# A list scheduler that draws 700 varied rankings, with step times taken from the trace

## The chip, the cores and the metric

The kernel runs on one core of a Trainium2 chip. The metric is the device time of one execution in microseconds (us), as the median of several runs. One core has five engines with a program each: PE (TensorE, matmuls; its weight loads are listed as PEld), DVE (VectorE), ACT (ScalarE), POOL (GpSimd) and SP, which here only issues DMAs. An engine runs its program in the written order and stops where an instruction waits for another engine or for a DMA.

## The reference

One layer of a diffusion transformer over 256 latent tokens x and 256 context tokens ctx, all of width 2048, in fp32. Cut to what matters:

```python
sh1, sc1, g1, sh2, sc2, g2 = split(silu(c) @ w_ada + b_ada, 6)      # 2048 x 12288, for c and for c_ctx
q, k, v (two head groups)  = (x * (1 + sc1) + sh1) @ w_in           # 2048 x 3072, context tokens likewise
heads = [window attention with a sink logit, global attention]      # rotary, qk-norm, keys of latent and context
x = layer_norm(ALPHA * x + g1 * (heads @ w_out))
u = x * (1 + sc2) + sh2
x = layer_norm(ALPHA * x + g2 * ((silu(u @ w_gate) * (u @ w_up)) @ w_down))   # hidden width 5632
```

## The kernel before

Every fp32 operand of a large product is split in two: `hi`, a cast on ACT, and `lo`, the rest, a subtraction on DVE (L537 and L540 in the first part, L268 and L269 in the FFN). `mm3` (L277 to L280) then makes one product of three matmuls of 128 x 512: hi by hi (L278), weights' lo (L279), input's lo (L280). So each MB of weights costs DMA time, ACT and DVE time and PE time together.

The first part goes up to about 392 us. It holds the modulation columns from w_ada (PE matmuls L588, and for one group of columns sums on DVE, `csum`, L650 and L652), the modulated input and its turn by PE (`uf`, `uh`, `ul`), the w_in products into `qacc` and `kvacc`, the rotary turns (`qrot`, `krot`) and the flips of q and k (L967, with `kTh`, `kTl` at L929), attention, the gate row `g1b` summed on DVE (L397), the w_out products with oTh and oTl, their finish (L1255, L1258, L1261), and the second modulation (`adav` L1117, columns L1413, x flips L1443, `u2h`, `u2l`). The FFN behind it is written out in a fixed order.

The order of the first part is made by the class `Flow`. Each operation is a step with an engine, an estimated time, the steps it comes after, and the buffers it takes and gives back: 4 `raw` and 2 `araw` tiles for loads, 4 pairs for hi and lo, 4 accumulators. `forward` simulates the engines with these estimates and lets each free engine start the ready step of lowest rank, `since` being the earliest time of a step. `backward` works out how late each step could start, and these times become the ranks of the next of 8 rounds; `run` keeps the plan that ends first and then issues all steps in that plan's order. The estimates exist only there: at run time an engine waits only for what its next instruction needs.

There are 56 filler steps on PE, of two matmul records each (`warm_step`, L1276, identity by identity), of last rank, so that the plan puts them where it sees PE idle.

Of the kernel before, what the change touches and what calls it, by code (L numbers as in the profile page):

```python
# [24 lines left out]
KD = D // P  # L25
# [10 lines left out]
NB = 512  # L36
# [13 lines left out]
COLD = 3  # L50
SLACK = 2500
# [23 lines left out]
class Flow:  # L75
# [8 lines left out]
    ROUNDS = 8  # L84

# [98 lines left out]

    def run(self):
        best, end = None, math.inf
        for _ in range(self.ROUNDS):
            order, last = self.forward()
            if not order:
                break  # L190
            if last < end:
                best, end = [(s, s.start, [b.pool for b in s.take]) for s in order], last
            late = self.backward(last)
            for i, s in enumerate(self.steps):
                s.rank = (late[s], i)
        assert best, "no step can start"
        for s, s.start, pools in best:
            for b, b.pool in zip(s.take, pools):
                pass
            s.fn()  # L200
# [3 lines left out]
def dit_layer(ctx: ExitStack, tc: tile.TileContext, x, c, cx, c_ctx, w_ada, b_ada, w_in, q_norm_g,  # L204
# [250 lines left out]
    def const_tables():  # L455
        nc.gpsimd.tensor_scalar_mul(nsink, sinkb, -1.0)
        for t in range(NT):
            for g, cg, sg in ((gq, cosQ, sinQ), (gk, cosK, sinK)):
# [19 lines left out]
             {"SP": 1300.0, "PE": 5600.0, "ACT": 5000.0, "DVE": 4000.0, "POOL": 4000.0})  # L478
    pools = {"raw": wraw, "araw": araw}
# [67 lines left out]
    def flow_seed(ps, src, after):  # L547
# [6 lines left out]
        return F.add("ACT", 475, fn, after, [ps])  # L554

    def flow_products(hl, deps, ready, cols, ps, xs, first, last, prev):
# [14 lines left out]
        return F.add("PE", 688 * len(cols), fn, after, [ps] if first and not seed else [], list(hl.rooms))  # L571
# [3 lines left out]
    def flow_columns(c0, ncol, shift, scale, ats, at):  # L575
# [18 lines left out]
        for g in range(ns):  # L594
            F.at = ats[g]
            ns1 = nk / 4 * (40 + 1.67 * width)
            if not c0:
                for i, k, m, since in ((0, 0, KD, 7200.0), (1, 0, KD // 2, 9700.0), (1, KD // 2, KD // 2, 11300.0)):
# [7 lines left out]
            if c0:  # L606
# [4 lines left out]
                prev = F.add("PE", 2 * ns1 + 420, both, [l0, l1, prev], [bank] if g == 0 else [], [r0, r1])  # L611
# [24 lines left out]
    def flow_vector_columns(c0, ncol, shift, scale, ats, at):  # L636
# [17 lines left out]
        for g in range(ns):  # L654
# [9 lines left out]
            for i in range(nk):  # L664
                for s in range(2):
                    last[s] = F.add("DVE", 1215, lambda s=s, g=g, i=i, raw=raw: term(s, g, i, raw), [ld, last[s]],
# [50 lines left out]
    def flow_part(k0, n, at, each):  # L717
# [20 lines left out]
        if k0:  # L738
            for load, room in ((load_x, []), (load_cx, [cx_room])):
                a = F.add(issue, 500 if issue == "ACT" else max(ns, 500), load, take=room, since=9300.0)  # L740
                loads.append((a, -4500) if issue == "ACT" else a)
        for s in range(2):
# [3 lines left out]
            for j0 in range(0, n, 2):  # L746
# [28 lines left out]
                if k0:  # L775
                    p = F.add("PE", 205 * nj, flip, [loads[s], copy], [ps], [cx_room] if s else [])
# [52 lines left out]
    def flow_blocks(g, bs, where=("raw", "araw")):  # L829

        k0, n = GROUPS[g]
        if n == 1:
            for i, (b0, m) in enumerate(((2, 1), (0, 2), (3, 2), (5, 1))):
                F.at = bs[0] + (bs[1] - bs[0]) * i / 4
                piece, = flow_weights(w_in, k0, 1, b0 * NB, m * NB, ("b4",), since=14000.0 if i and g == 0 else 0.0)
# [54 lines left out]
    def flow_keys(w):  # L890
# [10 lines left out]
        for r in range(4):  # L901
# [36 lines left out]
            a = F.add("PE", 210, flip, [a], [ps], [rot] if r < 2 else [])  # L938
# [6 lines left out]
    def flow_queries(gi):  # L945
# [8 lines left out]
        for t in range(NT):  # L954
# [28 lines left out]
            a = F.add("PE", 400, flip, [a], [ps], [rot])  # L983
# [784 lines left out]
```

## Time and profile before

| | |
|---|---|
| median of 3 runs | 1135.83 us (1132.12 to 1136.07) |
| profiled execution | 1135.22 us |
| its span in the trace | 1133.4 us |
| granted TensorE clock, mean | 0.995 |
| PE busy | 1110.8 us, 98% |
| DVE busy | 864.6 us, 76% |
| ACT busy | 566.5 us, 50% |
| DMA | 321.26 MB, mean 283 GB/s |

The page cuts the span into 40 slices of 28.3 us. PE reads 9 tenths or more in all but the first (8) and the last (5), and DMA reads 9 or more in the first six and 7 or 8 in the next four. The chain that ended last is 80% PE, 10% DVE and 6% DMA. A row of the timeline gives start, duration, engine, line, operation, tiles, count, and in brackets the idle time just before it with what ended it.

### The profile page before, as it was taken

Reading aid. Unit: us, or ns where it says so; the run is one execution under the profiler, and the core shown is the slowest. Engines: PE = TensorE matmul, PEld = TensorE weight load, DVE = VectorE, ACT = ScalarE, POOL = GpSimd, SP = SyncE. Lnnn points to the kernel's source line nnn. Section 1 sums busy time; section 2 is a strip of 40 time slices with the busy share of each in tenths; the row PEclk is TensorE's granted clock in tenths of the full one; section 3 lists DMA queues with packets and bytes.
Section 4 is the critical chain, followed back from the end, with each engine's and each line's share of the span. In section 5 each row is a group of like instructions: output and inputs, shape, how many; then the busy total and the mean of one; then the engine's idle time right before and its main releaser. Section 6 shows DMA issues by size and latency. Waiting matters only on the chain.

```text
span 1133.4 us, 14188 instructions
## 1 busy us (share of the span) xinstructions
PE 1110.8 (98%) x5277; PEld 899.7 (79%) x5277; DVE 864.6 (76%) x1088; ACT 566.5 (50%) x820; POOL 40.4 (4%) x81
## 2 busy tenths in 40 slices
PE   8999999999999999999999999999999999999995
PEld 6766778787887688888888888888888878888884
DVE  3768998999998997877677557767767778675556
ACT  3344584877784365454564444454444443434441
POOL 1000040101200001000000000000000000000000
PEclk9999999999999999999999999999999999999998
DMA  9999998787999789989876767777777998887531
GB/s 300 383 390 397 384 347 312 247 292 244 333 337 387 279 296 346 347 294 343 282 204 223 249 223 226 247 243 249 225 244 276 312 341 285 321 278 246 194 135 74
DMA packets 186413, 321.26 MB, mean 283 GB/s; under 512 B 8764, under 2 KB 51164, under 8 KB 184039
## 3 DMA queue, kind: packets, MB, share of 16 engines
q1 hardware_dynamic: 184536, 319.25, 81.8%
q10 hardware_dynamic: 1808, 1.11, 0.4%
q8 instruction: 41, 0.67, 0.2%
q14 instruction: 28, 0.23, 0.1%
HBM read 304.07 MB, written 16.25 MB: 283 GB/s over the span
## 4 chain that ended last, share of the span: by engine, by line
PE 80%; DVE 10%; DMA 6%; issue 2%; SPq 1%; ACT 1%; DVEq 0%; ACTq 0%
PE acc L278 24%; PE acc L280 24%; PE acc L279 24%; DMA raw<-in_w_in_dram 3%; DMA raw<-in_w_ada_dram 3%; DVE lo L540 2%; PE wk L1064 2%; PE wk L588 1%; DVE csum L652 1%; DVE g1b L397 1%; SPq L514 1%; DVE adav L397 1%; DVE hx L1046 1%; PE wk L278 0%; DVE xt L1677 0%
## 5 line engine op out<-in xcount | busy, mean ns | idle before, releaser
L269 DVE TENSOR_TENSOR lo<-raw,hi 128x1024 fp32r<-128x1024 f32 x258 | 311.8, 1220 | 176.1 <-ACT hi L268 172.5
L268 ACT CAST hi<-raw 128x1024 fp32r<-128x1024 f32 x258 | 270.5, 1055 | 321.5 <-PE acc L280 279.6
L280 PE MATMUL acc<-hi,u2l 128*128 128x512 f32 x704 | 274.1, 389 | 1.2 <-DVE u2l L1592 1.2
L278 PE MATMUL acc<-hi,u2h 128*128 128x512 f32 x704 | 274.4, 390 | 0.0
L279 PE MATMUL acc<-lo,u2h 128*128 128x512 f32 x704 | 274.1, 389 | 0.0
L280 PEld LDWEIGHTS acc<-hi,u2l 128*128 128x128 f32 x704 | 132.1, 188 | 29.6 <-DVE u2l L1592 2.1
L278 PEld LDWEIGHTS acc<-hi,u2h 128*128 128x128 f32 x704 | 132.1, 188 | 28.1 <-ACT u2h L1591 0.8
L279 PEld LDWEIGHTS acc<-lo,u2h 128*128 128x128 f32 x704 | 132.2, 188 | 27.0
L537 ACT CAST hi<-raw 128x1024 fp32r<-128x1024 f32 (+1 forms) x86 | 87.7, 1033 | 95.9 <-PE acc L280 48.9
L279 PE MATMUL acc<-lo,hTh 128*128 128x512 f32 x344 | 134.0, 390 | 0.5 <-DVE lo L269 0.5
L280 PE MATMUL acc<-hi,hTl 128*128 128x512 f32 x344 | 133.9, 389 | 0.0
L278 PE MATMUL acc<-hi,hTh 128*128 128x512 f32 x344 | 133.7, 389 | 0.0
L397 DVE SCALAR_TENSOR_TENSOR adav<-raw,cs,adav 128x512 f32<-128x512 f32 (+1 forms) x128 | 121.2, 947 | 7.7 <-DMA raw<-in_w_ada_dram 5.6
L540 DVE TENSOR_TENSOR lo<-raw,hi 128x1024 fp32r<-128x1024 f32 (+1 forms) x86 | 101.3, 1194 | 16.8 <-ACT hi L537 16.6
L278 PE MATMUL acc<-hi,uh 128*128 128x512 f32 x256 | 103.4, 404 | 1.5 <-ACT qacc L821 1.4
L279 PE MATMUL acc<-lo,uh 128*128 128x512 f32 x256 | 100.1, 391 | 0.1
L280 PE MATMUL acc<-hi,ul 128*128 128x512 f32 x256 | 100.1, 391 | 0.0
L279 PEld LDWEIGHTS acc<-lo,hTh 128*128 128x128 f32 x344 | 64.6, 188 | 14.5 <-DVE lo L269 1.0
L280 PEld LDWEIGHTS acc<-hi,hTl 128*128 128x128 f32 x344 | 64.6, 188 | 13.4
L278 PEld LDWEIGHTS acc<-hi,hTh 128*128 128x128 f32 x344 | 64.5, 188 | 13.4
L278 PEld LDWEIGHTS acc<-hi,uh 128*128 128x128 f32 x256 | 48.1, 188 | 18.6 <-issue 4.6
L280 PEld LDWEIGHTS acc<-hi,ul 128*128 128x128 f32 x256 | 48.0, 188 | 10.8 <-DVE ul L772 0.4
(224 smaller groups left out, 1195.6 us busy)
## 6 DMA issues: line engine op xcount, KB each, us to landing
raw<-in_w_ada_dram SPq DMA_DIRECT2D x63, 1024.0 KB, 7.8
raw<-in_w_gate_dram SPq DMA_DIRECT2D x44, 1024.0 KB, 5.4
raw<-in_w_up_dram SPq DMA_DIRECT2D x44, 1024.0 KB, 5.6
raw<-in_w_down_dram SPq DMA_DIRECT2D x44, 1024.0 KB, 6.0
raw<-in_w_ada_dram SPq DMA_DIRECT2D x66, 512.0 KB, 6.2
raw<-in_w_in_dram SPq DMA_DIRECT2D x18, 1024.0 KB, 10.0
raw<-in_w_out_dram SPq DMA_DIRECT2D x16, 1024.0 KB, 7.8
pd<-hx SPq DMA_DIRECT2D x64, 128.0 KB, 3.8
```

The source lines that it names most:

```text
L268: nc.scalar.copy(hi[:, :n], raw[:, s : s + n])
L269: nc.vector.tensor_tensor(lo[:, :n], raw[:, s : s + n], hi[:, :n].bitcast(F32), op=ALU.subtract)
L278: nc.tensor.matmul(ps, lhsT=xh, rhs=w[0], start=first, stop=False, skip_group_check=seeded)
L279: nc.tensor.matmul(ps, lhsT=xh, rhs=w[1], start=False, stop=False, skip_group_check=seeded)
L280: nc.tensor.matmul(ps, lhsT=xl, rhs=w[0], start=False, stop=last, skip_group_check=seeded)
L397: nc.vector.scalar_tensor_tensor(a[:, c : c + piece], raw[:, f : f + piece], cs[:, 4 * (g * (G4 * NB // w) + j) + 2, None], a[:, c : c + p ...
L514: nc.sync.dma_start(room.t.rearrange("p (k n) -> p k n", k=nk), w[k0 * P : (k0 + nk) * P, c0 : c0 + width].rearrange("(k p) n -> p k n", p=P),
L537: nc.scalar.copy(hl.hi[:, :n], raw.t[:, s : s + n])
L540: nc.vector.tensor_tensor(hl.lo[:, :n], raw.t[:, s : s + n], hl.hi[:, :n].bitcast(F32), op=ALU.subtract)
L588: nc.tensor.matmul(bank.t[32 * j : 32 * j + 32, :width], lhsT=cs[:, 4 * k + 2 - 2 * i : 4 * k + 34 - 2 * i], rhs=raw.t[:, c * width : (c + ...
L652: nc.vector.scalar_tensor_tensor(a, src, cs[:, k, None], a, op0=ALU.mult, op1=ALU.add)
L1064: nc.tensor.matmul(o_ps.t[:, : 2 * P].rearrange("p (g q) -> p g q", q=32), lhsT=v, rhs=pv[:, k], start=k == 0, stop=k == 3)
```

## The change

It touches what the planner is told and how long it looks. After the 8 rounds, `run` takes the best ranks 700 times, varies those of one stretch of the plan (noise on 30% of its steps, or a common shift for one engine), plans again and keeps the plan if it ends no later than the best. Step times are set anew: the accumulator seed on ACT 475 to 519, a product 688 to 685 per block, column sums and gate sums on DVE 1215 to 1197, and so on. SP begins at 2300 and not 1300. The two halves of the second load of w_ada may start from 9900 and 11900 (before 9700 and 11300), the first casts from 16300 (before 14000), the loads of x and ctx that ACT issues from 13000 and 22000 (before 9300), and a step on SP, which issues nothing, stands for the time of such a load. No wait, no buffer and no instruction is added or removed: each engine's program holds the same instructions as before. All lines shift by 33 (L1276 is L1309, L588 is L621, L278 is L311).

```diff
+    TRIES = 700
...
+    def plan(self):
+        order, last = self.forward()
+        if order and last <= self.end:
+            self.end, self.rank = last, [s.rank[0] for s in self.steps]
+            self.best = [(s, s.start, [b.pool for b in s.take]) for s in order]
+            return True
+        return False
...
     def run(self):
...
+        draw = random.Random(SEED)
+        for _ in range(self.TRIES):
+            ranks = list(self.rank)
+            a, w, d = draw.uniform(0, self.end), draw.uniform(2e3, 4e4), draw.gauss(0, 3e3)
+            near = [i for i, r in enumerate(ranks) if a <= r <= a + w]
+            kind, e = draw.random(), draw.choice(self.ENGINES)
+            for i in near:
+                if kind < 0.6:
+                    ranks[i] += draw.gauss(0, 3e3) if draw.random() < 0.3 else 0
+                else:
+                    ranks[i] += d if self.steps[i].eng == e else 0
+            self.give_ranks(ranks)
+            if self.plan() and draw.random() < 0.3:
+                self.late_ranks(self.end)
+                self.plan()
...
-             {"SP": 1300.0, "PE": 5600.0, "ACT": 5000.0, "DVE": 4000.0, "POOL": 4000.0})
+             {"SP": 2300.0, "PE": 5600.0, "ACT": 5000.0, "DVE": 4000.0, "POOL": 4000.0})
...
-        return F.add("ACT", 475, fn, after, [ps])
+        return F.add("ACT", 519, fn, after, [ps])
...
-                a = F.add(issue, 500 if issue == "ACT" else max(ns, 500), load, take=room, since=9300.0)
-                loads.append((a, -4500) if issue == "ACT" else a)
+                a = F.add(issue, 500 if issue == "ACT" else max(ns, 500), load, take=room, since=X_FROM.get(k0, 0.0))
+                loads.append(F.add("SP", ns, lambda: None, [(a, -1000)]) if issue == "ACT" else a)
```

What moves is the order. The first place is PE's start, up to the first w_in product (`acc<-hi,uh`). The fillers are `wk<-ident`, the column matmuls `wk<-raw,cs`, the x flips `wk<-ident,xt`. Before:

```order
3 L1276 MATMUL wk<-ident 128x128 x5
4 L588 MATMUL wk<-raw,cs 32x128 x16
5 L1276 MATMUL wk<-ident 128x128 x3
...
7 L1276 MATMUL wk<-ident 128x128 x2
8 L756 MATMUL wk<-ident,xt 128x128 x2
...
11 L1276 MATMUL wk<-ident 128x128 x4
...
13 L1276 MATMUL wk<-ident 128x128 x3
14 L622 MATMUL wk<-sel,ada 128x4
15 L1276 MATMUL wk<-ident 128x128 x11
16 L278 MATMUL acc<-hi,uh 128x512
```

And with the change:

```order
3 L1309 MATMUL wk<-ident 128x128 x8
4 L621 MATMUL wk<-raw,cs 32x128 x16
...
6 L1309 MATMUL wk<-ident 128x128 x3
7 L789 MATMUL wk<-ident,xt 128x128 x2
8 L1309 MATMUL wk<-ident 128x128 x3
...
10 L1309 MATMUL wk<-ident 128x128 x12
...
12 L1309 MATMUL wk<-ident 128x128 x6
...
14 L1309 MATMUL wk<-ident 128x128 x3
15 L655 MATMUL wk<-sel,ada 128x4
16 L1309 MATMUL wk<-ident 128x128 x12
17 L311 MATMUL acc<-hi,uh 128x512
```

28 fillers stand ahead of the first product before and 47 with the change. Of the others, 20 stood in one block behind 294 products before and 8 alone; with the change 3, 1, 2, 1 and 2 stand between early products.

The second place is DVE around the last flips of k: `kTl` is what the PE flip of q behind them waits for, and `g1b` sums wait for loads of w_ada. Before:

```order
119 L397 SCALAR_TENSOR_TENSOR g1b<-raw,cs,g1b 128x1024
120 L540 TENSOR_TENSOR lo<-raw,hi 128x1024 x2
121 L397 SCALAR_TENSOR_TENSOR g1b<-raw,cs,g1b 128x1024 x3
122 L929 TENSOR_TENSOR kTl<-wk,kTh 128x2x128 x4
123 L397 SCALAR_TENSOR_TENSOR g1b<-raw,cs,g1b 128x1024
```

And with the change:

```order
132 L1009 TENSOR_TENSOR qTl<-wk,qTh 128x4x128
133 L962 TENSOR_TENSOR kTl<-wk,kTh 128x2x128
134 L430 SCALAR_TENSOR_TENSOR g1b<-raw,cs,g1b 128x1024 x2
135 L573 TENSOR_TENSOR lo<-raw,hi 128x1024
136 L962 TENSOR_TENSOR kTl<-wk,kTh 128x2x128
137 L430 SCALAR_TENSOR_TENSOR g1b<-raw,cs,g1b 128x1024
138 L573 TENSOR_TENSOR lo<-raw,hi 128x1024
139 L962 TENSOR_TENSOR kTl<-wk,kTh 128x2x128 x2
```

The four kTl no longer stand in one block behind three gate sums.

The third place is PE's end of the first part, from the last w_out products (oTh, oTl) to the first product of the FFN (u2h, u2l). Before:

```order
1303 L1117 MATMUL wk<-ones,adav 128x2 x8
1304 L278 MATMUL acc<-hi,oTh 128x512
...
1364 L1413 MATMUL wk<-raw,cs 32x512 x4
1365 L1443 MATMUL wk<-ident,xt 128x128 x4
1366 L1413 MATMUL wk<-raw,cs 32x512 x12
```

And with the change:

```order
1366 L313 MATMUL acc<-hi,oTl 128x512
1367 L1150 MATMUL wk<-ones,adav 128x2 x8
1368 L1446 MATMUL wk<-raw,cs 32x512 x4
1369 L1476 MATMUL wk<-ident,xt 128x128 x2
1370 L1446 MATMUL wk<-raw,cs 32x512 x12
1371 L311 MATMUL acc<-hi,u2h 128x512
```

The eight `adav` matmuls stood 60 products ahead of the last product; now they stand behind it, and two of the four x flips stand 12 products ahead of it.

## Rows read from the trace of the kernel before

**Rows 1.** The page: span and busy time of each engine.

```profile
span 1133.4 us, 14188 instructions
...
PE 1110.8 (98%) x5277; PEld 899.7 (79%) x5277; DVE 864.6 (76%) x1088; ACT 566.5 (50%) x820; POOL 40.4 (4%) x81
```

**Rows 2.** Waits of PE: line waited for, total, times, longest (us).

```profile
PE wk L967 <- DVE kTl L929: 2.6, 1, 2.6
PE acc L278 <- ACT qacc L821: 1.4, 1, 1.4
PE acc L280 <- DVE u2l L1592: 1.2, 1, 1.2
```

**Rows 3.** Timeline of PE, 379 to 388 us (start, us, engine, line, ...).

```profile
379.81 0.39 PE L279 MATMUL acc<-lo,oTh 128*128 128x512 f32 x1
...
387.52 0.39 PE L280 MATMUL acc<-hi,oTl 128*128 128x512 f32 x1
```

**Rows 4.** Timeline of PE, the three long gaps between neighbours.

```profile
25.99 0.39 PE L280 MATMUL acc<-hi,ul 128*128 128x512 f32 x1
27.80 0.50 PE L278 MATMUL acc<-hi,uh 128*128 128x512 f32 x1 [1.42 <-ACT qacc L821]
...
199.74 0.39 PE L280 MATMUL acc<-hi,ul 128*128 128x512 f32 x1
202.74 0.66 PE L967 MATMUL wk<-ident,qrot 128*128 128x128 f32 x4 [2.62 <-DVE kTl L929]
...
392.47 0.40 PE L279 MATMUL acc<-lo,u2h 128*128 128x512 f32 x1
394.06 0.50 PE L280 MATMUL acc<-hi,u2l 128*128 128x512 f32 x1 [1.20 <-DVE u2l L1592]
```

**Rows 5.** Timeline of PE, the first product and the filler block.

```profile
17.88 0.47 PE L278 MATMUL acc<-hi,uh 128*128 128x512 f32 x1
...
118.00 4.62 PE L1276 MATMUL wk<-ident 128*128 128x128 f32 x40
122.38 0.48 PE L278 MATMUL acc<-hi,uh 128*128 128x512 f32 x1
```

**Rows 6.** Timeline of ACT, 20 to 28 us.

```profile
26.64 0.62 ACT L537 CAST hi<-raw 128x512 fp32r<-128x512 f32 x1 [5.77 <-DMA raw<-in_w_in_dram]
```

**Rows 7.** Timeline of DVE, the column sums, 90 to 137 us.

```profile
90.85 1.42 DVE L650 TENSOR_SCALAR csum<-raw,cs 128x1024 f32<-128x1024 f32 x2 [1.53 <-DMA raw<-in_w_ada_dram]
...
127.21 9.65 DVE L652 SCALAR_TENSOR_TENSOR csum<-raw,cs,csum 128x1024 f32<-128x1024 f32 x8
136.78 1.21 DVE L540 TENSOR_TENSOR lo<-raw,hi 128x1024 fp32r<-128x1024 f32 x1
```

**Rows 8.** Timeline of SP's queue, the loads of the column sums.

```profile
82.26 1.01 SPq L387 DMA_DIRECT2D raw<-in_w_ada_dram  x2
```

**Rows 9.** Stretches of the span: us, busy by engine (x), PEclk, DMA share, GB/s.

```profile
75.00:100.00 25.00, 25.00 (x137) 18.79 (x140) 20.05 (x26) 18.48 (x30) 0.00 (x0) 1.00 1.05 392
125.00:150.00 25.00, 24.80 (x135) 18.14 (x134) 25.00 (x27) 16.37 (x28) 4.83 (x5) 1.00 1.00 358
200.00:225.00 25.00, 22.38 (x106) 17.44 (x105) 24.06 (x44) 20.36 (x52) 3.29 (x12) 1.00 0.68 235
```

**Rows 10.** Timeline of DVE, 192 to 203 us.

```profile
192.99 1.28 DVE L397 SCALAR_TENSOR_TENSOR g1b<-raw,cs,g1b 128x1024 f32<-128x1024 f32 x1 [2.24 <-DMA raw<-in_w_ada_dram]
...
201.07 1.28 DVE L397 SCALAR_TENSOR_TENSOR g1b<-raw,cs,g1b 128x1024 f32<-128x1024 f32 x1 [0.24 <-DMA raw<-in_w_ada_dram]
202.28 1.41 DVE L929 TENSOR_TENSOR kTl<-wk,kTh 128x256 fp32r<-128x256 f32 x4
```

**Rows 11.** Timeline of DVE, 392 to 395 us.

```profile
392.47 1.21 DVE L540 TENSOR_TENSOR lo<-raw,hi 128x1024 fp32r<-128x1024 f32 x1
393.59 0.75 DVE L1592 TENSOR_TENSOR u2l<-uf,u2h 128x256 fp32r<-128x256 f32 x2
```

**Rows 12.** Timeline of PE, a column block at 71 us.

```profile
71.59 1.92 PE L588 MATMUL wk<-raw,cs 128*32 128x512 f32 x16
```

More of the change, by code (lines that the diff above doesn't have):

```diff
@@ L183, in backward, with give_ranks, late_ranks @@
         return start
+    def plan(self):
[5 more added lines that the diff above has]
+        return False
+    def give_ranks(self, ranks):
+        for i, (s, r) in enumerate(zip(self.steps, ranks)):
+            s.rank = (r, i)
+    def late_ranks(self, end):
+        late = self.backward(end)
+        self.give_ranks([late[s] for s in self.steps])
     def run(self):
-        best, end = None, math.inf
+        self.best, self.end = None, math.inf
         for _ in range(self.ROUNDS):
@@ L190, in run @@
                 break
[L191 to L197, printed above, removed]
+            self.plan()
+            self.late_ranks(last)
+        assert self.best, "no step can start"
+        draw = random.Random(SEED)
[12 more added lines that the diff above has]
+                self.late_ranks(self.end)
+                self.plan()
+        for s, s.start, pools in self.best:
             for b, b.pool in zip(s.take, pools):
@@ L570, in flow_products @@
         after = [deps[0], (deps[1], 200), ready[0], (ready[1], 400), prev]
-        return F.add("PE", 688 * len(cols), fn, after, [ps] if first and not seed else [], list(hl.rooms))
+        return F.add("PE", 685 * len(cols), fn, after, [ps] if first and not seed else [], list(hl.rooms))
     last_load = []
@@ L609, in both @@
                     fn(g, 1, r1, 0, nk)
[L611 removed]
+                prev = F.add("PE", 2075, both, [l0, l1, prev], [bank] if g == 0 else [], [r0, r1])
         F.at = at
@@ L665, in flow_vector_columns @@
                 for s in range(2):
-                    last[s] = F.add("DVE", 1215, lambda s=s, g=g, i=i, raw=raw: term(s, g, i, raw), [ld, last[s]],
+                    last[s] = F.add("DVE", 1197, lambda s=s, g=g, i=i, raw=raw: term(s, g, i, raw), [ld, last[s]],
                                     [sums[s]] if g == i == 0 else [], [raw])
@@ L775, in flow_part @@
                 if k0:
-                    p = F.add("PE", 205 * nj, flip, [loads[s], copy], [ps], [cx_room] if s else [])
+                    p = F.add("PE", 40 + 205 * nj, flip, [loads[s], copy], [ps], [cx_room] if s else [])
                 else:
@@ L834, in flow_blocks @@
                 F.at = bs[0] + (bs[1] - bs[0]) * i / 4
-                piece, = flow_weights(w_in, k0, 1, b0 * NB, m * NB, ("b4",), since=14000.0 if i and g == 0 else 0.0)
+                piece, = flow_weights(w_in, k0, 1, b0 * NB, m * NB, ("b4",), since=CAST_FROM if i and g == 0 else 0.0)
                 for j in range(m):
@@ L982, in flow_queries @@
             ropes[gi, t] = a
-            a = F.add("PE", 400, flip, [a], [ps], [rot])
+            a = F.add("PE", 450, flip, [a], [ps], [rot])
             a = F.add("ACT", 475, cast, [a, *(c for c, _ in qT[gi][1])], rooms if t == 0 else [])
@@ L1171, in flow_vector @@
             for i in range(G4 * NB // min(w, 2 * NB)):
-                last = F.add("DVE", 1215, lambda g=g, i=i, room=room: vector_sum(room.t, a, w, g, i), [ld, last], give=[room])
+                last = F.add("DVE", 1197, lambda g=g, i=i, room=room: vector_sum(room.t, a, w, g, i), [ld, last], give=[room])
         F.at = span[1]
@@ L1267, in finish @@
             a = F.add("DVE", 710, base, [(a, 80)])
-            outs[n, t] = F.add("DVE", 710, spread, [(a, 80)])
+            outs[n, t] = F.add("DVE", 620, spread, [(a, 80)])
         for t in range(NT):
```

12 lines of the change are left out of this document (8 added, 4 removed).

## The prediction

> **What bounds the kernel now.** I read the page first. PE is busy for 1110.8 of 1133.4 us [rows 1], so at most 22.6 us of the span can be PE standing idle, and the start and the end of the program take part of that. The waits of PE come next, since a new order of the same instructions can only save what an engine stands still for. Three of them lie in the first part, which the planner orders: 2.6 us on kTl, 1.4 us on qacc and 1.2 us on u2l, 5.2 us together [rows 2]. The rest of the waits lies at the start, ahead of everything that moves, or in the FFN, whose order stays.
>
> A busy row of a product is 0.39 us long though the next begins after less: from 379.81 to 387.52 lie 34 spacings, 7.71 / 34 = 0.227 us each [rows 3]. So a wait shows shorter than it costs, and I take each gap from start to start, less 0.227 us [rows 4]:
> - 25.99 to 27.80: 1.81 - 0.23 = 1.58 us (qacc).
> - 199.74 to 202.74: 3.00 - 0.23 = 2.77 us (kTl).
> - 392.47 to 394.06: 1.59 - 0.23 = 1.36 us (u2l).
>
> Together 5.7 us. The Trainium skill, Trainium Kernel Development and Optimization, Performance Expectations, says that matmul busy time is a bad metric because matmuls are pipelined. The trace agrees with it, by the rows of 0.39 us at a spacing of 0.227 us; a reader who went by busy time would look for up to 22.6 us, or count 5.2 us.
>
> Then DVE and DMA. From 125 to 150 us DVE is busy for all 25.00 us, and the DMA engines for all of the time too [rows 9]. The column sums begin at 90.85 us, when their load lands, and run with the `lo` between them to 136.78 us [rows 7]; that load was issued at 82.26 us [rows 8] and the transfers move 392 GB/s in that stretch [rows 9]. So between 91 and 137 us the pace is DVE's, and the filler block at 118.00 us [rows 5] stands where PE was ahead of it.
>
> **The change, part by part.** The numbers that are edited reach no instruction; they move the order. Each engine has the same instructions, so the work on PE is the same, and the sum has only stalls in it.
>
> *Fillers.* The block at 118.00 us holds 40 records, 20 fillers, and takes 122.38 - 118.00 = 4.38 us, 0.219 us each [rows 5]. With the change 19 more of them stand ahead of the first product: 19 x 0.219 = 4.2 us, so I put it at 17.88 + 4.2 = 22.1 us. All 56 are spent by 122 us in both orders, so this by itself is 0: what PE gives early it gets back at 118. It is 0 only if DVE is not late there. Between 22 and 118 us PE runs some 4 us behind its former place less the 1.58 us, and whatever PE frees comes free so much later.
>
> *The qacc gap, -1.58.* ACT stood 5.77 us for a load of w_in before the cast at 26.64 us, and the copy of qacc that PE needed is next in its program [rows 6]. In the changed order of SP the fourth w_in piece stands behind 4.7 MB of loads and not behind 6.0 MB; 1.3 MB at 392 GB/s [rows 9] are 3.3 us, and PE comes 4 us later besides. I take the whole 1.58 us.
>
> *The kTl gap, -2.77.* DVE did four kTl at 202.28 us, behind a gate sum that began at 201.07 us, when its load landed, and PE's flip of q waited for them [rows 10]. In the changed order they stand one, one and two between the sums, and PE's flips of q and k are spread between products. So the block of 1.41 us is gone, and of the loads only a part is ahead of the first kTl. I take all of it here, and give back what DVE lacks under new waits.
>
> *The u2l gap, -1.36.* At 392.47 us DVE still had a `lo` of 1.21 us ahead of u2l [rows 11], since the finish of the last products had begun just as PE needed it. With the change eight adav matmuls stand between the last product and the columns, and PE has some 2 us more to do there. I take the whole gap.
>
> *Switches, -0.4.* A product behind another kind of matmul shows 0.50 us and not 0.39 [rows 4], 0.11 us more. The changed order has 72 such switches in place of 76: 4 x 0.11 = 0.4 us.
>
> *The x loads and first casts.* The loads are issued by ACT at the same places in its program or behind other work of PE's that waits anyway; 28 fillers covered this before, 47 do now. I cost it at 0. Without that cover a late flip of x would delay the first product one for one.
>
> *New waits, +2.0.* With 5.7 us of stalls gone, PE asks for each `lo` and kTl earlier. I walked DVE's program: time of each instruction less the work that stands ahead of it, against the moment that PE would need it with no stall. Before, the column sums held DVE at 41.2 us (start minus work ahead) from 114 to 141 us; the changed order allows 37.9 at the `lo` of 136 to 142, which is 3.3 us less. For it the sums must begin some 4 us earlier, at about 87 us. SP issues 29.4 MB ahead of their first load and not 30.9: 1.5 MB / 392 GB/s = 4.0 us earlier [rows 9]. That just serves; a wait of 0 to 1.5 us stays. At the kTl before, DVE stood at 49.0, and the change allows 45.2, 3.8 us less; my walk gives 45.4 to 47, so 0 to 2 us. Each wait shifts PE and lessens the later ones, so these do not add: 0 from below, 3.8 us from above, if DVE is no earlier anywhere. I take 2.0, the upper part of the walk, since the g1b loads come two at a time and DVE stood 2.24 us for one at 192.99 us [rows 10].
>
> The sum: -1.58 - 2.77 - 1.36 - 0.4 + 2.0 = -4.1 us. Against the profiled execution (1135.22 us, span 1133.4 and 1.8 us around it) this is 1131.1 us; the median, 1135.83, is 0.6 us above that execution, so as a median **1131.7 us**, with 1129.7 to 1133.5 as this case's own range.
>
> **The rivals.**
>
> *All of it (1129.7 or less).* DVE keeps up everywhere, new waits 0: 6.1 us, and up to 1 us more from gaps too small for the list. For it speaks that the load order is 4.0 us ahead where 3.3 are needed. Against: DVE had no idle in 125 to 150 us [rows 9].
>
> *DVE no earlier.* The first column sum again begins at 90.85 us, PE meets DVE at the same instants as before, and 3.8 us come back as waits on `lo` between 118 and 142 us or on kTl. Gain 6.1 - 3.8 = 2.3 us: 1133.5 us. For it: the stretch is full of transfers at 392 GB/s, so a load does not land earlier by being asked for earlier.
>
> *Slower: buffers come free late.* The four raw tiles are freed by PE's column matmuls among others. A block of them began at 71.59 us [rows 12] behind 156 products; the changed order puts that block behind 168, 12 x 0.227 = 2.7 us, and 17 fillers more stand ahead of it, 3.7 us, so at about 78 us. Three later blocks stand 30, 18 and 24 products further back. If a raw tile is missing when SP comes to the load of 82.26 us [rows 8], SP's queue stops with all loads behind it, and the column sums begin later than before. With y us later than 90.85 the waits are 3.8 + y, and the sum is -2.3 + y: slower than before from y = 2.3, so from a first sum after 93.2 us. For y = 6 (the lateness of the block) it is +3.7, so 1139.5 us. Against it: the tile of that load had been freed by DVE, not by PE.
>
> *The clock.* The longest wait, 2.77 us, stands in a stretch whose granted clock is 1.00, so the upper level of 2.4 GHz [rows 9]. A longer one, now that no fillers stand behind 122 us, could let it fall to the lower level, 1.2 GHz: a product would then take 2 x 0.227 us, and if it stayed for 18 of them (I take as many as fit into 4.1 us) they cost 4.1 us more, 1135.8 us with my forecast. The Trainium skill, TensorE: Matmul & The Clock Gate, Part 1: The HAM clock gate, says that PE's clock falls to half after idling; no wait in these rows was long enough to show it.
>
> That the change does nothing is out, since all three engines' orders move.
>
> **How the numbers follow.** Forecast 0.46; all of it 0.20; DVE no earlier 0.19; buffers late 0.12; the clock 0.03. About 0.5% of the time, 5.7 us, is what a measurement of this kernel can tell from no change: 1130.2 and 1141.5 us. Faster than that: all of it, and a little of the forecast's lower edge, 0.23. Slower: buffers late with y over 8, or a chain of such waits, 0.08. Else 0.69. The range goes from 1128.5 (all of it and the small gaps) to 1138.0 (buffers late with y = 4.5), leaving 0.07 below and 0.10 above.
>
> **What would show it.** Right: the first product near 22 us, no gap at 26 to 28, none over 1 us on kTl or u2l, the first column sum near 87 us, one or two new waits on `lo` or kTl of 2 us together. DVE no earlier: PE waits on `lo` L573 between 118 and 142 us of 3 us or more. Buffers late: SP's queue waiting for PE before its loads of 85 to 95 us, and the first sum after 93 us. It would be wrong from the ground if the FFN moved too: its order is the same, so its length, from the first u2 product to the end, must be the same within 1 us.

## The result and the profile after

The changed kernel takes 1140.65 us as a median of 6 runs (1138.65 to 1141.87), the kernel before 1134.45 us on the same chip (6 runs, 1132.12 to 1136.07). The ratio is 1.005, 95% interval 1.0036 to 1.0064: slower by about 6 us. The forecast was 1131.7 us with a range of 1128.5 to 1138.0 us, so both its direction and its range were wrong.

The page of the profiled execution of the changed kernel, first the span and PE, as in [rows 1]:

```profile
span 1139.0 us, 14157 instructions
...
PE 1113.9 (98%) x5277; PEld 901.1 (79%) x5277; DVE 865.3 (76%) x1088; ACT 566.5 (50%) x820; POOL 37.4 (3%) x81
```

The span has grown by 5.6 us and PE's busy time by 3.1 us. The busy shares tell nothing of where. The waits of PE, in the columns of [rows 2]:

```profile
PE wk L621 <- DMA raw<-in_w_ada_dram: 1.8, 2, 1.4
PE acc L311 <- ACT u2h L1624: 1.4, 1, 1.4
...
PE acc L313 <- DVE oTl L1108: 0.8, 1, 0.8
PE wk L313 <- DVE qTl L1009: 0.7, 1, 0.7
PE wk L655 <- ACT ada L650: 0.7, 1, 0.7
```

All three waits of [rows 2] are gone from this trace: PE no longer stands for qacc, kTl or u2l (in a second trace of this kernel, told of below, it stands 1.0 us for kTl, ahead of another matmul). In their place are waits for the loads of a column block (L621 was L588), for u2h, and several of under 1 us.

A row of the table below is a piece of PE's program between two products, counted from the start. "Standing" is worked out from the two traces: for each pair of neighbouring matmuls the distance of their starts, less the lower quartile of that distance for the same two kinds of matmul over the traces of this study. "Work" is the sum of those quartiles.

| products | before: standing, work | after: standing, work | change of standing |
|---|---|---|---|
| up to the first | 5.1, 9.7 us | 5.1, 14.0 us | 0 |
| 1 to 60 | 5.0, 16.9 | 3.1, 15.2 | -1.8 |
| 60 to 300 | 11.8, 63.5 | 10.9, 64.7 | -0.9 |
| 300 to 390 (116 to 150 us) | 3.0, 28.3 | 7.7, 25.3 | +4.7 |
| 390 to 720 | 4.8, 83.8 | 2.8, 83.7 | -2.0 |
| 720 to 960 | 4.0, 89.3 | 5.6, 90.6 | +1.6 |
| 960 to 1200 (332 to 412 us) | 6.5, 71.3 | 9.2, 70.4 | +2.7 |
| the FFN behind | 2.9, 711.4 | 2.9, 711.4 | 0 |

The sum of standing rises by 4.3 us, that of work by 1.0 us (other neighbours, not more matmuls); from the start of the last matmul to the end the changed kernel takes 0.3 us more (13.4 against 13.1 us), and together this is the 5.6 us. The gains that were forecast are there (-1.8 and -2.0; in the second trace of the changed kernel -1.0 and -0.2), and are outweighed by 300 to 390, 720 to 960 and 960 to 1200. At product 720 the two traces are level (235.64 us before, 235.79 after; 237.13 in the second trace): up to there gains and losses cancel. At product 1200 the changed kernel is 5.3 us late (406.30 and 411.61 us).

The place that lost most, in PE's timeline of the changed kernel:

```profile
132.25 0.39 PE L313 MATMUL acc<-hi,ul 128*128 128x512 f32 x1
134.03 1.92 PE L621 MATMUL wk<-raw,cs 128*32 128x512 f32 x16 [1.39 <-DMA raw<-in_w_ada_dram]
136.66 1.05 PE L655 MATMUL wk<-sel,ada 128*128 128x4 f32 x8 [0.71 <-ACT ada L650]
138.06 1.09 PE L789 MATMUL wk<-ident,xt 128*128 128x128 f32 x8 [0.35 <-DMA xt<-in_x_dram]
139.44 1.05 PE L789 MATMUL wk<-ident,cxt 128*128 128x128 f32 x4 [0.29 <-DMA cxt<-in_ctx_dram]
140.14 0.77 PE L311 MATMUL acc<-hi,uh 128*128 128x512 f32 x1
140.72 0.63 PE L312 MATMUL acc<-lo,uh 128*128 128x512 f32 x1
141.14 0.63 PE L313 MATMUL acc<-hi,ul 128*128 128x512 f32 x1
```

PE waits for the last column block's load, then does short matmuls with a gap ahead of each, because no products stand between them. Behind it the products come 0.42 us apart (140.72 to 141.14) and not 0.227 us.

### The profile page after: what moved, and what is told of

It reads as the page before. It is cut to its first block, busy times and chain, and to the rows that moved or that the text cites. A ratio compares the mean times of both kernels' runs of the same rounds, so it can differ in the third digit from the quotient of the medians.

```text
span 1139.0 us, 14157 instructions
## 1 busy us (share of the span) xinstructions
PE 1113.9 (98%) x5277; PEld 901.1 (79%) x5277; DVE 865.3 (76%) x1088; ACT 566.5 (50%) x820; POOL 37.4 (3%) x81
## 4 chain that ended last, share of the span: by engine, by line
PE 87%; DVE 5%; DMA 4%; ACT 1%; issue 1%; SPq 0%; DVEq 0%; ACTq 0%
PE acc L311 26%; PE acc L313 26%; PE acc L312 26%; DMA raw<-in_w_ada_dram 2%; PE wk L621 2%; PE wk L1097 2%; PE wk L1309 1%; DVE adav L430 1%; DMA cxt<-in_ctx_dram 1%; PE wk L789 1%; DMA pd<-hx 1%; PE wk L311 1%; PE wk L313 1%; DVE lo L573 1%; PE wk L312 0%
## 5 line engine op out<-in xcount | busy, mean ns | idle before, releaser
L311 PE MATMUL acc<-hi,u2h 128*128 128x512 f32 x704 | 274.4, 390 | 1.4 <-ACT u2h L1624 1.4
L311 PEld LDWEIGHTS acc<-hi,u2h 128*128 128x128 f32 x704 | 132.2, 188 | 29.4 <-ACT u2h L1624 2.3
L312 PEld LDWEIGHTS acc<-lo,u2h 128*128 128x128 f32 x704 | 132.2, 188 | 27.1
L311 PE MATMUL acc<-hi,hTh 128*128 128x512 f32 x344 | 133.7, 389 | 0.0
L311 PE MATMUL acc<-hi,uh 128*128 128x512 f32 x256 | 103.9, 406 | 0.0
L313 PEld LDWEIGHTS acc<-hi,hTl 128*128 128x128 f32 x344 | 64.6, 188 | 13.4
L311 PEld LDWEIGHTS acc<-hi,hTh 128*128 128x128 f32 x344 | 64.5, 188 | 13.4
L311 PEld LDWEIGHTS acc<-hi,uh 128*128 128x128 f32 x256 | 48.6, 190 | 15.6 <-issue 4.8
```

The costliest lines, as they stand in the source:

```text
L311: nc.tensor.matmul(ps, lhsT=xh, rhs=w[0], start=first, stop=False, skip_group_check=seeded)
L312: nc.tensor.matmul(ps, lhsT=xh, rhs=w[1], start=False, stop=False, skip_group_check=seeded)
L313: nc.tensor.matmul(ps, lhsT=xl, rhs=w[0], start=False, stop=last, skip_group_check=seeded)
```

## The experiments

All ratios are to the kernel before, run beside each kernel on its chip. The medians of the kernel before in these comparisons lie between 1132.98 and 1134.78 us, so ratios are compared, and the changed kernel's is 1.005 [1.0036, 1.0064]. It was run once more unaltered.

> The changed kernel once more, unaltered, as the measure for the runs beside it: 1138 to 1141 us, ratio to before 1.005.

It gave 1140.57 us, ratio 1.0055 [1.0039, 1.0072].

### The two halves of the change

New step times and starts without the draws, and the draws with the old step times and starts:

```diff
-    TRIES = 700
+    TRIES = 0
```

> The new step times and earliest starts alone, no varied rankings. If the varied rankings lose the time (they keep orders that fit the planner's simulation too closely), this is near before: 1133 to 1137 us, ratio 0.997 to 1.003. If the new step times and starts lose it (the second MB of w_ada ahead of the halves is in this order too), 1138 to 1142 us.

> The 700 varied rankings alone, with the step times and earliest starts of before. If the varied rankings lose the time: 1138 to 1143 us. If the new step times and starts lose it: 1130 to 1136 us.

The first gave 1136.98 us, ratio 1.0022 [1.0011, 1.0034], the second 1137.98 us, ratio 1.0031 [1.0017, 1.0046]. By the numbers given, the first lies in the range for guilty draws (1133 to 1137 us) and the second a little under its own (1138 to 1143 us). But both intervals lie above 1, so neither guess of one guilty half holds: each loses. That 0.22% and 0.31% come near the 0.50% and 0.55% measured for both does not show that the two losses add, since each kernel has stalls of its own. One thing in the first expectation was not so: in the trace of the first run the second MB of w_ada is issued at 9.13 us, behind the two halves, as in the kernel before. The second run exchanged stalls: the kTl wait is gone, and this line of PE's waits is new.

```profile
PE wk L311 <- DVE qTl L1009: 3.8, 1, 3.8
```

Then another draw:

```diff
-SEED = 3
+SEED = 1
```

> The changed kernel with another seed of the 700 draws. If the loss comes from what the planner leaves out (buffers that free late, tiles laid over each other at the end, the clock), another draw loses too: 1137 to 1143 us. If seed 3 was an unlucky draw, 1130 to 1135 us.

1136.14 us, ratio 1.0013 [1.0001, 1.0025]. So about 0.4% of the 0.55% hangs on the draw. But the other draw does not win either: its PE stands 2.0 us ahead of the first u2 product as in the changed kernel, and 2.05 us ahead of an x flip at 135 us.

### Fillers

Only the first 28 of the 56 fillers are issued:

```diff
-        warm(wps.t, 1)
+        if i < KEEP:
+            warm(wps.t, 1)
```

> The changed kernel's order, but only the first 28 of the 56 filler steps are issued (fillers compute nothing that is used). Theory one, late buffers: the fillers ahead of 87 us push PE's column blocks back, these free the raw tiles late, SP stands and the DMA engines run short at 35-40, 55-65 and 70-75 us. Then: first product near 18 us (22.1 now), column block at 71.6 now near 66, 70-75 us above 350 GB/s (233 now), first column sum at 87 to 89 us (91.35 now), no wait over 1 us at 117 to 135 us, and 1132 to 1136.5 us. Theory two, the fillers stand where PE would wait anyway: first product near 18 us too, but PE then waits some 4 to 6 us for casts or lo before 91 us or for loads at 117 to 140 us, DMA as now, and 1139.5 to 1141 us.

1141.13 us, ratio 1.0068 [1.0054, 1.0082]: the time of theory two. With 5.5 us less work PE stood 5.4 us more (worked out as in the table). Both theories had expected the first product near 18 us, and it came at 20.96 us:

```profile
17.41 0.39 PE L656 MATMUL wk<-sel,ada 128*128 128x4 f32 x2 [0.39 <-ACT ada L651]
20.96 0.80 PE L312 MATMUL acc<-hi,uh 128*128 128x512 f32 x1 [3.17 <-ACT uh L803]
```

It waited for uh, whose work begins with a copy on ACT. In the changed kernel:

```profile
18.66 0.27 ACT L650 COPY ada<-wk 128x128 f32<-128x128 f32 x1 [6.96 <-PE wk L621]
```

Before, this copy was at 14.64 us. It follows the column matmuls of two halves of a load of w_ada, which began at 12.10 and 13.93 us before and at 15.84 and 17.95 us with the change. On SP's queue 2 MB of w_ada stand ahead of these halves in the changed order, and 1 MB before, but PE's list has no wait for either half. What stands ahead of them on PE are fillers: 10 and 14 before, 26 and 32 with the change. 18 more fillers at 0.219 us are 3.9 us, and the copy is 4.0 us later. With the first 28 fillers kept, 26 and 28 still stand there, so this run left in place most of what makes the first product late. Its wait for uh also let the granted clock fall:

```profile
20.00:25.00 5.00, 4.04 (x10) 3.21 (x11) 4.14 (x7) 3.25 (x7) 0.00 (x0) 0.50 1.15 316
```

The products came 0.43 us apart there, and product 60 at 42.09 us, against 40.68 with all fillers. So a part of what PE stood more is the slow clock, and the run does not decide between the two theories.

Next the other 28 fillers were put back, in one block ahead of the last column block (the edit above, and `warm_up(ps.t, 28)` in `both` of the last block):

> As the run with 28 fillers, but the other 28 are issued in one block just ahead of the last column block (at 132 us now), so that PE's work is the changed kernel's to the last record. Theory one, late buffers: loads as in the run with 28 fillers, first column sum at 87 to 89 us, the block of 6.1 us takes the place of the waits at 132 to 140 us and of the slow clock behind them, and 1134.5 to 1138.5 us. Theory two: the loads land no earlier, the block comes on top of waits earlier on, and 1140 to 1143 us.

1143.41 us, ratio 1.0086 [1.0071, 1.0101]. The last loads of w_ada are issued no earlier (121.19 us, 121.28 in the changed kernel), and the block of 6.4 us takes the place of a part of the waits only: product 390 came at 151.56 us, 1.9 us later than in the changed kernel. The time lies above both ranges. As in the run before, 26 and 28 fillers stand ahead of the two halves.

### The load order at the start

```diff
+        sp = [i for i, e in enumerate(best) if e[0].eng == "SP" and e[0].ns > 0]
+        best.insert(sp[7], best.pop(sp[1]))
```

> The changed kernel's order with one load moved on SP: the second MB of w_ada goes behind the first four w_in pieces, so that the two halves and the first w_in piece land 1 MB sooner, as before; and 28 of the 56 fillers are issued, spread over PE's start as before. Theory three: the first product came at 21 to 22 us with 28 fillers as with 56 because the load order puts 1 MB ahead of the two halves of w_ada (1 MB at some 290 GB/s is 3.6 us), and all that PE frees comes so much later. Then: copy of ada at 14.5 to 15.5 us (18.66 now), first product at 17.5 to 19 us, column block at 71.6 now at 67 to 69, first column sum at 87 to 90 us, and 1134.5 to 1137.5 us. Rival: the stages behind 60 us are bound by loads and by the order on DVE whatever the start does: first product near 18 us, but product 330 within 1 us of the changed kernel's 125.7 us, and 1139 to 1141 us.

1140.51 us, ratio 1.0058 [1.0038, 1.0077]. The first product came at 19.97 us, product 330 at 124.87 us against 125.67: the rival, the time is that of the changed kernel, though the first product was not as early as either side had expected, and the copy of ada came at 16.95 us, not at 14.5 to 15.5, so theory three fails at its first sign. The run says something of the fillers too: with the first product 2.1 us sooner than in the changed kernel, the column blocks of 57.83, 64.03 and 71.59 us began only 0.3 us sooner, and 27.1 MB had been moved by 80 us, against 26.9. The runs spread from 1137.6 to 1145.2 us, more than of any other kernel, so a small gain stays open; the profiled execution is the fastest of them.

### The slow clock

16 fillers more in PE's gaps between 132 and 140 us:

```diff
+                    if ncol == 4 and c0 == 8 * P and g == ns - 1:
+                        ps.t = wk_bank()
+                        warm_up(ps.t, 6)
```

(and 6 ahead of the turn, 2 ahead of each of two flips)

> The changed kernel's order plus 16 fillers in the gaps that PE has between 132 and 140 us (6 ahead of the last column block, 6 ahead of its turn, 2 ahead of each of two flips; 3.5 us of matmuls whose result is overwritten). Theory: the granted clock fell to 0.50 at 140-142 us because PE was sparsely used, and the products of 140.1 to 142.9 us at 0.43 us spacing and the flips before them cost 1.3 to 2 us; with the fillers the clock stays 1.00 and the time is 1138.6 to 1139.6 us. Rival: the clock stays down or what follows waits for DVE anyway: 1140 to 1142 us.

The granted clock of 125 to 150 us went from 0.93 to 1.00. The stretch in the changed kernel and in this one (columns as in [rows 9]):

```profile
125.00:150.00 25.00, 22.26 (x118) 16.75 (x117) 24.57 (x26) 14.79 (x25) 0.00 (x0) 0.93 0.96 342
```

```profile
125.00:150.00 25.00, 24.95 (x155) 20.09 (x154) 24.26 (x26) 15.76 (x27) 0.50 (x2) 1.00 0.99 354
```

Product 390 came 1.2 us sooner (148.37 us against 149.62) and stayed so up to product 900 (309.44 against 310.54), and then the lead was gone: product 1020 at 357.14 us against 356.25. The time is 1140.89 us, ratio 1.0063 [1.0048, 1.0077]. The clock's price here is about 1 us in these two traces; it does not reach the end.

### Column blocks moved by hand

```diff
+        for g, n in enumerate((3, 4, 3, 3)):
+            move(f"col4_{g}", n)
```

(`move` puts a step of PE ahead of n product steps; the fourth stood as early as it could)

> The changed kernel with three column blocks of PE moved ahead and nothing else: those at 57.8, 64.0 and 71.6 us stand 18, 24 and 18 products sooner (96, 108 and 138 products ahead of them in place of 114, 132 and 156; 93 to 150 in the kernel before). Theory four: it is the place of these blocks among the products, not the fillers and not the first load, that frees the raw tiles late, starves the DMA engines at 55-65 and 70-75 us (332, 363 and 233 GB/s) and makes the loads of the last column blocks late, so that PE stands and its clock falls at 117 to 143 us. Then 55-75 us above 370 GB/s, first column sum at 88 to 89.5 us (91.35 now), the gap ahead of the last column block (1.55 us) under 0.5, and 1136 to 1139 us. Rival: the holes only move, or the blocks stand for their own loads; the gap at 132 us stays over 1 us and the time is 1139.5 us or more.

1141.56 us, ratio 1.0058 [1.0044, 1.0071]: the rival. The DMA engines no longer run short at 55 to 70 us (388 to 403 GB/s), but at 75 to 80 us (192 GB/s against 398). The hole has moved.

> The changed kernel with three column blocks of the last group moved ahead on PE: those at 108.8, 118.2 and 134.0 us stand 18, 12 and 6 products sooner (258, 294 and 354 ahead of them). Theory five: each of these blocks frees the raw tiles into which the loads of the block after it go (loads issued at 108.5 and 121.3 us, just as the block before them ends), so a late block makes the next late: PE's gaps at 117 and 132 us (0.58 and 1.55) and the bare stretch behind them (block, turn, flips, 1.29 and 0.5 us gaps, clock 0.50 at 140 to 142 us) are one chain. Then loads of the last block issued near 117 us, no gap over 0.5 us at 110 to 136 us, clock 1.00 in 125 to 150 us, product 390 at 145.5 to 147 us (149.6 now), and, if nothing later is the bound, 1136 to 1138 us. Rival: product 390 comes sooner as in theory five, but what PE gains here it gives back at later waits (attention, w_out) as in the run with 16 fillers more, and the time is 1139.5 to 1141 us.

```diff
+        for g, n in ((1, 3), (2, 2), (3, 1)):
+            move(f"col8_{g}", n)
```

1142.06 us, ratio 1.005 [1.0031, 1.007]. Theory five is wrong: the last loads are issued at 121.7 us as before, the gap of 1.55 us is exchanged for one of 2.8 us ahead of the block before it, and product 390 is no sooner (150.69 us).

> As the run with the three blocks moved, and the buffers of two loads of the last columns exchanged (as in the run on the end of the first part, but without moving the adav matmuls). Theory five and the end together: product 390 at 145.5 to 147 us, gap ahead of the first u2 product under 1 us (2.0 now), and 1134.5 to 1137 us. Rival, given back later: 1138.5 to 1141 us.

1140.13 us, ratio 1.0043 [1.0027, 1.006]: no clear change either. The gap ahead of the first u2 product is gone, but product 390 came at 151.75 us, later than in the changed kernel, so the half of it that was theory five failed again. Here, too, the order of the FFN's first part came out different.

### The end of the first part

The adav matmuls moved 8 product steps earlier:

```diff
+        move("m0", 8)
```

> The changed kernel's order, but the eight adav matmuls (L1150), the two DVE copies behind them and POOL's combine stand 8 product steps (48 products) earlier. Theory: the 2.0 us that PE stands at 396.4 us is the chain adav matmuls - DVE - POOL (395.1 us) - ACT uf - u2h, so the wait falls to 0.5 us or less and the time to 1138.4 to 1139.3 us. Rival: DVE's finish or ACT set it; PE's wait moves to u2l and the time is 1140 to 1141 us.

1141.78 us, ratio 1.0073 [1.0058, 1.0089]. The theory was wrong: POOL was done at 385 us, and PE stood for u2h 1.4 us as before. What ACT waits for is shown by its timeline, in the changed kernel:

```profile
397.06 0.81 ACT L1622 ACTIVATE uf<-wk,mB,mA 128x128 f32<-128x128 f32 x2 [6.17 <-PE wk L1446]
```

The tile `uf` belongs to a pool that is laid over the first part's `araw` tiles. Before, the first two column loads lay in the two araw tiles; in the changed plan the first and the last do, so uf waits for the last of the column matmuls. The exchange of two buffers tests it:

```diff
+        best[one], best[last] = (a, t, q), (b, u, p)
```

> The changed kernel with two things moved at the end of the first part: the adav matmuls, DVE's copies and POOL's combine 8 product steps earlier (as in the run that moved these alone, where PE still stood 1.4 us), and the buffers of two loads of the last columns exchanged, so that the first and second block of column matmuls (L1446) read the two araw tiles, as before, and not the first and the last. Theory: uf is written where an araw tile lay, so ACT waited for the last of the 12 column matmuls to read it. Then uf starts behind the second block, some 1.8 us sooner, PE's gap ahead of the first u2 product falls from 2.0 us (start to start, less the spacing) to under 0.8, and the time falls by 1.2 to 1.8 us against the changed kernel. Rival: u2h waits for something else; the gap stays over 1.3 us and the time is the same.

The gap went, in ACT's and PE's timelines of this kernel:

```profile
395.77 0.81 ACT L1641 ACTIVATE uf<-wk,mB,mA 128x128 f32<-128x128 f32 x2 [1.41 <-PE wk L1465]
```

```profile
395.95 2.78 PE L1465 MATMUL wk<-raw,cs 128*32 128x512 f32 x24
398.67 0.50 PE L327 MATMUL acc<-hi,u2h 128*128 128x512 f32 x1
```

From 395.95 us to the first u2 product are 2.7 us, as before the change, and 4.2 us in the changed kernel: theory right for the gap. But the time is 1143.31 us, ratio 1.0068 [1.005, 1.0087]. Here, as with the adav matmuls moved alone, the order of the FFN's first part came out different too, and products 1200 to 1800 took 140.1 us in place of 137.8, so the time cannot be read as the price of the gap.

### The kernel before, changed by one move

Two moves that take away the two largest stalls of the kernel before:

```diff
+        late = [e for e in best[: k[0]] if e[0].tag == "gate"][-3:]
...
+        best[at:at] = late
...
+        best.insert(max(cast, first(copy)), copy)
```

> The kernel before with two moves by hand and nothing else: three gate sums on DVE go behind the four kTl, and ACT's copy of qacc goes ahead of the cast that waits for a load at 26.6 us. Theory: stalls of one place can be taken away without giving them back, where the rest of the order stays. The kTl gap (2.78 us) falls to under 0.6 us, the qacc gap (1.58 us) to under 1, and the time is 2 to 4 us under before (ratio 0.9965 to 0.998). Rival: what follows is bound by DVE or by loads; the gaps go and others of the same size open within 100 us, ratio 0.9995 to 1.001.

1135.24 us, ratio 1.0008 [0.9999, 1.0017]: the rival. The waits for kTl and for qacc of [rows 2] are gone from PE's list, which now has these:

```profile
PE wk L299 <- DVE qTl L998: 0.8, 1, 0.8
...
PE wk L723 <- DVE part L1150: 0.5, 1, 0.5
PE acc L297 <- DVE qacc L845: 0.5, 1, 0.5
```

Product 630 was 1.3 us sooner than before, product 1200 0.7 us, product 1800, in the FFN, 0.2 us. No stall as long as the old ones opened: the gain goes bit by bit. 4.4 us of stalls taken away by hand bought nothing that can be measured.

Then the one thing that the prediction had costed at nothing, in the kernel before: its 20 fillers of 118 us go ahead of the first product.

```diff
-        warm(wps.t, 1)
+        warm(wps.t, 21 if i == 27 else 1 if i < 36 else 0)
```

> The kernel before with one thing moved: its block of 20 fillers at 118 us is issued ahead of the first product instead (as in the changed kernel, where 47 of 56 stand there). Each engine's instructions and the order of all others stay; the first product and the column blocks of PE come 4.4 us later. Theory six: late column blocks free the raw tiles late, the DMA engines fall short between 25 and 80 us, and what is short at 80 us is never made up, since they run at 390 to 397 GB/s from there to 130 us in every kernel. All runs of the changed order had moved 26.4 to 27.1 MB by 80 us, the kernel before 28.6. Then: under 27.8 MB by 80 us, a gap of 2 us or more at 100 to 142 us, and 1136 to 1139 us. Rival, as the prediction had it: fillers cost nothing early and come back at 118 us, over 28.2 MB by 80 us, and 1133 to 1135.5 us.

1136.48 us, ratio 1.0021 [1.0007, 1.0035]: theory six, with its numbers. Stretches of the kernel before, of this one and of the changed kernel (the last column is GB/s):

```profile
25.00:50.00 25.00, 23.58 (x217) 17.84 (x216) 17.14 (x30) 9.17 (x16) 0.00 (x0) 1.00 1.07 378
50.00:80.00 30.00, 30.00 (x173) 19.63 (x172) 17.87 (x26) 11.69 (x18) 0.00 (x0) 1.00 1.05 394
80.00:100.00 20.00, 20.00 (x105) 14.34 (x107) 17.02 (x21) 15.09 (x26) 0.00 (x0) 1.00 1.05 391
100.00:130.00 30.00, 30.00 (x171) 22.18 (x164) 28.82 (x25) 12.08 (x19) 0.00 (x0) 1.00 1.05 395
```

```profile
25.00:50.00 25.00, 25.00 (x212) 19.76 (x214) 17.92 (x28) 9.39 (x16) 0.00 (x0) 1.00 1.02 359
50.00:80.00 30.00, 30.00 (x185) 19.17 (x178) 19.07 (x28) 9.48 (x13) 0.00 (x0) 1.00 1.02 372
80.00:100.00 20.00, 20.00 (x105) 15.31 (x105) 15.51 (x21) 14.68 (x25) 0.00 (x0) 1.00 1.05 387
100.00:130.00 30.00, 28.88 (x145) 20.08 (x143) 28.26 (x24) 15.72 (x24) 0.00 (x0) 1.00 1.05 394
130.00:145.00 15.00, 12.78 (x63) 9.61 (x64) 15.00 (x16) 6.75 (x10) 0.00 (x0) 0.89 1.05 393
```

```profile
25.00:50.00 25.00, 25.00 (x225) 19.26 (x224) 18.40 (x31) 11.03 (x20) 0.00 (x0) 1.00 1.06 365
50.00:80.00 30.00, 30.00 (x164) 19.32 (x163) 18.65 (x26) 7.55 (x10) 0.00 (x0) 1.00 0.96 352
80.00:100.00 20.00, 20.00 (x111) 15.52 (x110) 17.34 (x22) 15.35 (x26) 0.00 (x0) 1.00 1.05 397
100.00:130.00 30.00, 29.59 (x145) 21.39 (x144) 29.27 (x26) 14.54 (x22) 0.00 (x0) 1.00 1.04 388
130.00:145.00 15.00, 12.26 (x64) 8.71 (x63) 15.00 (x16) 8.26 (x14) 0.00 (x0) 0.89 0.95 335
```

Summed from the start of the span (rate times length; the first 25 us are 7.3, 6.9 and 7.2 MB), the kernel before has moved 28.6 MB by 80 us, this one 27.0 and the changed one 26.9 MB. From 80 to 130 us all run at 387 to 397 GB/s and nothing is made up: 1.6 MB are 4.1 us at 394 GB/s. In this kernel the first column sum came at 94.90 us, 4.05 us later than in [rows 7], and PE stood for the last column block's load:

```profile
132.22 1.79 PE L588 MATMUL wk<-raw,cs 128*32 128x512 f32 x8 [3.35 <-DMA raw<-in_w_ada_dram]
```

The changed kernel's second run, the nine kernels made from its order and the one with TRIES 0 had all moved between 26.4 and 27.1 MB by 80 us; seed 1 had 27.7, the draws with the old times 28.0, the two moves in the kernel before 28.4. So no move by hand took the shortfall out of the changed order, and none made it faster beyond its interval. The MB alone do not give the time either: the draws with the old times lost 0.31% with 28.0 MB, more than TRIES 0 with 27.0 (0.22%).

The traces also show how lateness and stalls take each other up. This kernel is 4.3 us later than the kernel before at product 390 (151.27 and 146.96 us), but only 1.2 us at product 630 (210.52 and 209.30), since the wait for kTl, 2.6 us in [rows 2], is gone from its list: PE came too late to stand for it.

## Why the prediction was wrong

**New waits, +2.0: the step that failed.** The prediction looked for them on `lo` and kTl, by DVE's program alone, and took 2.0 us. In the table the places with new standing are +4.7, +1.6 and +2.7 us, 9.0 together: a load of w_ada for PE's column block, the bare stretch behind it with the clock at half, oTl, qTl, u2h. DVE's pace was not the limit in the first of them; the load was. Loads for PE, the waits of attention and of the w_out products, and the tile under `uf` had no term in the sum. Why the load is late in the changed kernel stays open: the runs that moved column blocks only moved its wait, and none was faster beyond its interval.

**Fillers, costed at 0: wrong in the kernel before, not shown to cost the changed kernel anything.** "So this by itself is 0: what PE gives early it gets back at 118." With the fillers alone moved PE does get their time back: the first half of the last column block began at 127.81 us, and at 128.01 before. What does not come back is what waits for PE meanwhile, and this costs 0.21%, some 2.4 us (the last run). SP's queue shows how. This is the issue of the w_ada load that the second half of that block waited for, before and with the fillers moved:

```profile
120.26 0.37 SPq L514 DMA_DIRECT2D raw<-in_w_ada_dram  x1
```

```profile
124.58 0.37 SPq L514 DMA_DIRECT2D raw<-in_w_ada_dram  x1
```

It is 4.3 us later, as is the load of [rows 8] (86.54 us): the order of the loads is the same, SP waits for tiles that PE, now later, still reads, and the stretch behind has no spare rate (387 and 394 GB/s).

In the changed kernel the first product came at 22.11 us, as worked out, and PE had no wait of its list between 6.44 us and there, so the fillers ahead of it do set it. But no run shows that this costs the changed kernel time at the end: with 28 fillers, spread as before, and the load order at the start put back, the first product was 2.1 us sooner, the column blocks 0.3 us, and the time was that of the changed kernel within its interval (the run on the load order). SP's waits from 25 to 84 us, before and after the change, show that PE's column blocks are what it waits for there:

```profile
SPq L514 <- PE wk L588: 18.1, 11, 4.5
```

```profile
SPq L547 <- PE wk L621: 31.4, 10, 7.0
```

These are 13 us more, but its other waits are 12 us less (all together 42.0 and 43.0 us), so the rows show who holds the tiles and not how much is lost. That the changed kernel's shortfall, of the same size as that of the last run, costs it the same is not shown: none of the runs took it away from that order.

**The rival "buffers come free late" had a mechanism that the last run shows, and a deciding point that missed.** It was to decide when the first column sum came after 93.2 us. With the fillers moved in the kernel before that sum came at 94.90 us. In the changed kernel it came at 91.35 us, only 0.5 us later than before, since the change orders those loads sooner, and PE stood for a load of the last column blocks instead.

**The removed stalls: -1.58 and -2.77 right, as stalls.** PE stands 1.8 us less up to product 60 and 2.0 us less from 390 to 720 (in the second trace 1.0 and 0.2). That such a gain reaches the end was taken for granted. The run with the two moves shows it does not: both stalls gone, ratio 1.0008 [0.9999, 1.0017].

**The u2l gap, -1.36: wrong.** It went, and a gap of 2.0 us for u2h took its place (0.5 us lie there where PE does not wait). The tile laid over the araw tiles was not in the prediction at all, and the planner has no step for it.

**Switches, -0.4: wrong sign.** Fewer switches were counted, but the sum of usual spacings rose by 1.0 us.

**The clock rival** held in small: about 1 us, after a stretch that was sparse rather than idle. **"The FFN stays"** held: 2.9 us of standing in both.

What stays open: how the 0.55% divide between the shortfall, products 720 to 1140 and the end of the first part. From 720 to 1140 both traces of the changed kernel have waits of 0.8 us for oTl and 0.7 us for qTl that the kernel before does not have, and no run moved a step there: this is a rival that was not tried. Taking single ones away did not lower the time of this order, and the profiles of one kernel differ by 1 us and more in the attention part (products 600 to 720 stand 2.0 us in one trace of the changed kernel and 3.8 in the other).

## What to carry to other kernels

A plan that its own model calls earlier need not be earlier on the chip: here five plans of one planner (before, times only, draws only, two seeds of both) lie between 1 and 1.0055, each with other stalls, and none beats the plan that the rest of the kernel was built around. Before costing idle time or fillers at nothing, ask what is held meanwhile: a late reader holds its tiles, SP stands behind them, and transfers that were not started cannot be made up where the DMA engines are already full. Count the MB moved by the end of such a stretch, not only the waits in it, compare the time of the same product at several later places before a gain is booked, and give the planner a step for every later reader that takes over a buffer.

## What was not expected of the hardware

PE's granted clock fell without a wait as long as one that had left it up. In the changed kernel the longest single wait from 130 to 140 us is 1.39 us, and the clock of 140 to 142 us is 0.50, the lower level of 1.2 GHz; what went ahead were 8 us of short matmuls with gaps:

```profile
132.00:134.00 2.00, 0.64 (x3) 0.19 (x1) 2.00 (x2) 0.59 (x1) 0.00 (x0) 1.00 1.05 387
134.00:136.00 2.00, 1.92 (x16) 0.42 (x16) 2.00 (x3) 0.00 (x0) 0.00 (x0) 1.00 1.05 386
136.00:138.00 2.00, 1.05 (x8) 0.97 (x8) 2.00 (x3) 1.83 (x3) 0.00 (x0) 1.00 0.88 323
138.00:140.00 2.00, 1.65 (x11) 1.45 (x12) 2.00 (x3) 1.75 (x3) 0.00 (x0) 0.87 0.51 103
140.00:142.00 2.00, 2.00 (x8) 1.61 (x7) 2.00 (x4) 0.65 (x2) 0.00 (x0) 0.50 1.03 391
```

The wait of 2.77 us of [rows 4], with products on both sides, had left it at 1.00. The Trainium skill, TensorE: Matmul & The Clock Gate, Part 1: The HAM clock gate, says that the clock follows how busy PE has been of late; these rows agree, and the run with 16 fillers in the gaps kept it at 1.00. One wait can do it too: the clock fell behind the wait of 3.35 us in the last run (0.89 over 130 to 145 us) and behind that of 3.17 us in the run with 28 fillers (0.50 over 20 to 25 us).
